# Product banks of a seven-product block: both operand parts in one 512-column matmul, and weight sums placed one product earlier

## The chip, the cores and the metric

The kernel runs on one core of a Trainium2 chip. The metric is the device time of one execution in microseconds (us), which is some 2 us longer than the span from the first instruction to the last; the median of several runs is compared. The engines are named as in the profile: PE is the matrix engine (PEld its weight loads), DVE the vector engine, ACT the scalar engine, POOL the one that issues some DMAs, SP the one that issues most of them.

## The reference, cut to what matters

One decoder block of width 2048 over 512 tokens in float32: a normed input is multiplied by `w_in`, goes through two token mixers (latent attention and a gated spatial unit), the two are merged by gates, and a dense feed-forward layer follows.

```
f = rms_norm(h, norm_ffn_g[l])
h = h + (jax.nn.silu(f @ w_gate_ffn[l]) * (f @ w_up_ffn[l])) @ w_down_ffn[l]
```

The change touches the matrix products with the columns of `w_in` that make `u` and the two gate branches, and `f @ w_gate_ffn` and `f @ w_up_ffn`, which are 2048 by 5632 each.

## The kernel before

Each of those products is cut into jobs of 256 output features. The part called x-jobs here has 20 of them (4 for `u`, 16 for the gates), the feed-forward part has 44 (gate and up in turn). A job is one `Unit`. A unit does the product by a two-by-two block scheme with seven products in place of eight (Strassen's, in Winograd's form): the weights are four quarters `a11`, `a21`, `a12`, `a22`, some of which are first added to or subtracted from one another, and the inputs stand ready as seven sums for each of eight row pairs `kp`.

Every operand is held as two parts, a high part in the matmul's own format and the rest, the low part. A product of two operands is three matmuls: low weights by high input, high weights by high input, high weights by low input. `product` issues these three for each of the eight `kp`, 24 matmuls of 256 columns, all into one PSUM bank of which 256 of the 512 columns are used (`bank`). The high and the low input lie side by side, `x[:, :256]` and `x[:, 256:]`.

A unit has three banks. Products 0 and 4 go into the first (called a below), 1, 3 and 5 into the second (b), 2 and 6 into the third (d). The banks go on accumulating, and what stands in them is read between the products: `read(0)` copies bank a to `u` (ACT), `read(1)` adds bank b and `u` to `u2` (DVE), `read(3)` makes `c22` from banks b and d (DVE, two adds), `read(4)` copies bank a to `c11` (ACT), `read(5)` makes `c12` and `read(6)` makes `c21` (DVE). After `read(6)` the job's `finish` runs: in an x-job one activation on each of two tiles (ACT), in a gate job of the feed-forward two multiplications (DVE) and two Silu (ACT), in an up job two multiplications with the gate (DVE). A product into a bank has to wait until the read of that bank before it is through.

`weights(i)` makes the weights of product i: in `form_w` ACT casts the 128x1024 sum to the high part and DVE subtracts it from the sum for the low part. Before that, where needed, DVE makes the sum itself: three sums (`s1`, `a21`, `a11`) in `weights(1)`, one (`a12`) in `weights(5)`.

`run` sets the order by hand. Every instruction of a unit is pinned to program order on its engine, and one step `g` does `read` of product g-4, `weights` of product g, and the matmuls of product g-3. DVE and ACT therefore work through one list each, step by step, and an instruction that waits holds up all that is behind it on its engine. There is room for four pairs of weight parts, so the cast of product g can start when product g-4 is through on PE.

The rest of the kernel (the products with 512 columns in `gemm_fm` and `gemm_tm`, attention, the last projection) isn't touched.

Of the kernel before, what the change touches and what calls it, by code (L numbers as in the profile page):

```python
# [88 lines left out]
def tile_block(ctx: ExitStack, tc, a):  # L89
    nc = tc.nc  # L90
# [8 lines left out]
    def T():  # L99
        return af.get(2)  # L100

    def drop(*ts):

        for t in ts:
            if isinstance(t, (tuple, list)):
                drop(*t)
            elif id(t) in af.held:
                af.put(t)
            else:
                ar.put(t)  # L110

    def PS():
        return psp.tile([P, 512], F32, tag="b", name="b")
# [183 lines left out]
    kps = PS()  # L297
    for half in range(2):
# [5 lines left out]
        for k in range(8):  # L304
            w = wk[:, k].rearrange("p o m -> p (o m)")
# [61 lines left out]
    pin = tc.keep_in_program_order  # L367

    def form_w(src):
        hi, lo = ar.get(4), ar.get(4)  # L370
        hv, lv = (t.rearrange("p (k m) -> p k m", m=P) for t in (hi, lo))
        pin(nc.scalar.copy(hv, src))  # L372
        pin(nc.vector.tensor_tensor(out=lv, in0=src, in1=hv.bitcast(F32), op=ALU.subtract))  # L373
        return hi, lo

    FORM = (0, 5, 6, 4, 1, 2, 3)

    def product(ps, w, xs, kps, first):
        hi, lo = w
        for kp in kps:  # L380
            x = xs[kp]
            ks = slice(kp * P, (kp + 1) * P)
            xh, xl = x[:, :256], x[:, 256:]
            pin(nc.tensor.matmul(ps, lo[:, ks], xh, start=first and kp == 0, stop=False, skip_group_check=True))  # L384
            pin(nc.tensor.matmul(ps, hi[:, ks], xh, start=False, stop=False, skip_group_check=True))  # L385
            pin(nc.tensor.matmul(ps, hi[:, ks], xl, start=False, stop=kp == 7, skip_group_check=True))  # L386

    def bank():
        return PS()[:, :256]

    def plus(out, in0, in1):
        pin(nc.vector.tensor_tensor(out=out, in0=in0, in1=in1, op=ALU.add))  # L392

    def minus(out, in0, in1):
        pin(nc.vector.tensor_tensor(out=out, in0=in0, in1=in1, op=ALU.subtract))  # L395

    def copy(out, t):
        pin(nc.scalar.copy(out, t))  # L398

    class Unit:  # L400
# [8 lines left out]
            self.finish = finish  # L409

        def weights(self, i):
            if i == 0:
                return form_w(self.a11)
            if i == 1:
                self.st = af.get(4)
                self.s1 = self.st.rearrange("p (k m) -> p k m", m=P)
                plus(self.s1, self.a21, self.a22)
                minus(self.a21, self.a11, self.a21)
                minus(self.a11, self.s1, self.a11)
                return form_w(self.a11)  # L420
            if i == 2:
                return form_w(self.a21)
            if i == 3:
                w = form_w(self.s1)
                drop(self.st)
                return w
            if i == 4:
                return form_w(self.a12)
            if i == 5:
                minus(self.a12, self.a12, self.a11)  # L430
                return form_w(self.a12)
            w = form_w(self.a22)
            drop(self.raw)
            return w

        def multiply(self, i, w, fx, kps):
            if i == 0 and 0 in kps:
                self.banks = [bank() for _ in range(3)]
            n = FORM[i]
            xs = [f[n] if isinstance(f, list) else f[:, n * 512:(n + 1) * 512] for f in fx]  # L440
            product(self.banks[(0, 1, 2, 1, 0, 1, 2)[i]], w, xs, kps, i < 3)

        def read(self, i):
            ba, bb, bd = self.banks
            if i == 0:
                self.out = T(), T()
                self.u = T(), T()
                copy(self.u[0][:, :256], ba)
            u, u2 = self.u[0][:, :256], self.u[1][:, :256]
            (c11, c12), (c21, c22) = ((t[:, :256], t[:, 256:]) for t in self.out)  # L450
            if i == 1:
                plus(u2, bb, u)
            elif i == 3:
                plus(c22, bb, u)
                plus(c22, bd, c22)
            elif i == 4:
                copy(c11, ba)
            elif i == 5:
                plus(c12, bb, u)
            elif i == 6:  # L460
                plus(c21, bd, u2)
                drop(self.u)
                self.finish(self.out)

    def run(jobs, fx, rest, ends, lead=3):


        af.keep, af.pack = 32, True
        jobs = list(jobs)
        last = 7 * len(jobs) - 7  # L470
        units, ready = {}, {}

        def unit(n):
            if n < len(jobs):
                units[n] = Unit(*jobs[n])

        unit(0)
        for g in range(last + 7 + lead + 1):
            g1, g2 = g - lead, g - lead - 1
            if g2 >= 0:  # L480
                units[g2 // 7].read(g2 % 7)
            if g < last + 7:
                ready[g] = units[g // 7].weights(g % 7)
                if g % 7 == 6:
                    unit(g // 7 + 2)
            if g == lead - 1:
                rest = rest()
                next(rest)
                early = len(fx)
                for i in range(lead):  # L490
                    units[0].multiply(i, ready[i], fx, range(early))
                for _ in rest:
                    pass
                unit(1)
            if 0 <= g1 < last + 7:
                if g1 == last:
                    fx[:] = [ar.cut(f, 2) for f in fx]
                units[g1 // 7].multiply(g1 % 7, ready[g1], fx, range(early if g1 < lead else 0, len(fx)))
                drop(ready.pop(g1))
                if g1 >= last:  # L500
                    drop([f[FORM[g1 - last]] for f in fx])
                    if g1 - last in ends:
                        ends[g1 - last]()
        af.keep, af.pack, ar.keep = 0, False, 0
# [28 lines left out]
    def x_rest():  # L533
# [5 lines left out]

    latT, zs = [], []  # L540
    run(x_jobs(), fx, x_rest, {0: lambda: zs.append(lat_in(0)), 2: lambda: zs.append(lat_in(1)),
                               4: lambda: latT.append(latents(0, zs[0])), 5: lambda: latT.append(latents(1, zs[1]))})
    qnT, kvT = latT
# [119 lines left out]
    def k_proj(pr):  # L663
        ch = [chunk(a["w_ukv"][pr, c]) for c in range(2)]
        ks = []
        for m in range(2):
            ps = PS()
            for k in range(4):
                hi, lo = ch[k // 2]
                o = (k % 2) * 512 + m * P  # L670
                mm3(ps, hi[:, o:o + P], lo[:, o:o + P], *kvT[k], k == 0, k == 3)
            ks.append(split(ps))
        return ks, ch
# [63 lines left out]
    def values(e, pts, vs):  # L737
        ps = PS()
        for j, (ph, pl, q0) in enumerate(pts):
            vh, vl = vs[j // 2]  # L740
            o = (j % 2) * 256 + e * P
            mm3(ps[:, q0:], vh[:, o:o + P], vl[:, o:o + P], ph, pl, j == 0, j == NB - 1)
        return ps
# [15 lines left out]
    ks, ch = k_proj(0)  # L759
    vs = v_proj(ch)  # L760
    for pr in range(NP):
        prob, ptiles = scores(qs, qp, ks)
        if pr + 1 < NP:
            qs, qp = q_proj(pr + 1)
            ks, ch = k_proj(pr + 1)
# [12 lines left out]
        for e in range(2):  # L778
            ps = values(e, pts[e][1], vs)
            t = T()  # L780
# [60 lines left out]
    for c in range(4):  # L841
# [30 lines left out]
        if c == 0:  # L872
# [3 lines left out]
            for tb in range(NB):  # L876
                t = T()
# [56 lines left out]
    def split_hidden():  # L934
        hid[:4] = [move(t) for t in hid[:4]]

    run(ffn_jobs(), ff, f_rest, {1: lambda: hid.extend(hidden_in(0, 4)), 4: split_hidden,
                                 5: lambda: hid.extend(hidden(4, 4))})

# [32 lines left out]
    for c in range(4):  # L972
        t = T()
# [3 lines left out]
    for tb in range(NB):  # L977
        ts = slice(tb * P, (tb + 1) * P)
        for c in range(4):
            ps = PS()  # L980
            for k in range(4):
                xh, xl = hid[k]
# [6 lines left out]
        for c in range(4):  # L989
            t = h[tb][c]  # L990
# [87 lines left out]
```

## Time and profile before

| | |
|---|---|
| median of 3 runs | 2736.05 us (2734.65 to 2737.57) |
| the profiled execution, its own time | 2731.94 us |
| its span, first to last instruction | 2729.9 us |
| mean granted TensorE clock | 0.993 |
| PE busy | 2679.5 us, 98% of the span |
| DVE busy | 1731.3 us, 63% |
| ACT busy | 1093.6 us, 40% |
| instructions on PE | 17320 matmuls, of which 10752 are those of `product` |

The busy share of an engine is a mean over parts with different limits. A matmul's duration in the profile runs from its start to the modelled end, and the next one starts before that end, so the cost of a matmul in a row of them is the distance between two starts. In the timelines the start stands first, then the time that the group took; behind "x2" two neighbours of one form are merged. In brackets stands how long the engine was idle before and what released it.

### The profile page before, as it was taken

Reading aid. Unit: us, or ns where it says so; the run is one execution under the profiler, and the core shown is the slowest. Engines: PE = TensorE matmul, PEld = TensorE weight load, DVE = VectorE, ACT = ScalarE, POOL = GpSimd, SP = SyncE. Lnnn points to the kernel's source line nnn. Section 1 sums busy time; section 2 is a strip of 40 time slices with the busy share of each in tenths; the row PEclk is TensorE's granted clock in tenths of the full one; section 3 lists DMA queues with packets and bytes.
Section 4 is the critical chain, followed back from the end, with each engine's and each line's share of the span. In section 5 each row is a group of like instructions: output and inputs, shape, how many; then the busy total and the mean of one; then the engine's idle time right before and its main releaser. Section 6 shows DMA issues by size and latency. Waiting matters only on the chain.

```text
span 2729.9 us, 41675 instructions
## 1 busy us (share of the span) xinstructions
PE 2679.5 (98%) x17320; PEld 2458.8 (90%) x17320; DVE 1731.3 (63%) x2200; ACT 1093.6 (40%) x1534; POOL 201.4 (7%) x377
## 2 busy tenths in 40 slices
PE   8999999999899999999999999999999999999998
PEld 6879999998789878888799999999999998888887
DVE  5647777787677433333687887887888875344434
ACT  6334444457456422233544443444444343222212
POOL 1000000011101220001000000000000020000000
PEclk9999999999999999999999999999999999999999
DMA  7433343343423754334233232332322356334321
GB/s 300 150 125 114 119 146 125 130 144 129 139 86 124 250 188 147 120 112 139 101 123 118 110 131 109 131 111 107 140 109 109 132 170 224 123 123 132 112 89 62
DMA packets 104540, 365.22 MB, mean 134 GB/s; under 512 B 14304, under 2 KB 14304, under 8 KB 104352
## 3 DMA queue, kind: packets, MB, share of 16 engines
q1 hardware_dynamic: 72720, 260.60, 27.2%
q0 software_dynamic: 30192, 99.38, 10.6%
q8 instruction: 135, 2.21, 0.3%
q10 hardware_dynamic: 1440, 2.60, 0.3%
q14 instruction: 53, 0.43, 0.1%
HBM read 317.17 MB, written 45.35 MB: 133 GB/s over the span
## 4 chain that ended last, share of the span: by engine, by line
PE 82%; issue 9%; DMA 4%; DVE 3%; ACT 1%; POOL 1%; SPq 0%; POOLq 0%; ACTq 0%; DVEq 0%
PE b L384 15%; PE b L386 15%; PE b L385 15%; PE b L169 12%; PE b L171 12%; PE b L170 12%; DMA af<-in_xT 1%; DVE ar L373 1%; DMA af<-in_w_uq 1%; ACT ar L372 1%; DVE af L395 0%; PE b L732 0%; DVE af L392 0%; DMA sgd<-af 0%; DMA af<-in_w_lat 0%
## 5 line engine op out<-in xcount | busy, mean ns | idle before, releaser
L384 PE MATMUL b<-ar 128*128 128x256 f32 x3584 | 1017.6, 284 | 6.6 <-ACT ar L333 3.4
L386 PE MATMUL b<-ar 128*128 128x256 f32 x3584 | 1017.2, 284 | 5.4 <-DVE ar L119 5.4
L385 PE MATMUL b<-ar 128*128 128x256 f32 x3584 | 1016.5, 284 | 0.0
L169 PE MATMUL b<-ar 128*128 128x512 f32 (+1 forms) x2016 | 766.3, 380 | 25.3 <-ACT ar L154 11.6
L171 PE MATMUL b<-ar 128*128 128x512 f32 (+1 forms) x2016 | 763.8, 379 | 0.3 <-DVE ar L155 0.3
L170 PE MATMUL b<-ar 128*128 128x512 f32 (+1 forms) x2016 | 764.0, 379 | 0.0
L373 DVE TENSOR_TENSOR ar<-af,ar 128x1024 fp32r<-128x1024 f32 x448 | 543.2, 1223 | 267.9 <-ACT ar L372 266.9
L384 PEld LDWEIGHTS b<-ar 128*128 128x128 f32 x3584 | 690.5, 193 | 7.9 <-DVE af L392 4.0
L386 PEld LDWEIGHTS b<-ar 128*128 128x128 f32 x3584 | 690.5, 193 | 6.3 <-DVE ar L119 6.3
L385 PEld LDWEIGHTS b<-ar 128*128 128x128 f32 x3584 | 690.7, 193 | 0.1
L372 ACT CAST ar<-af 128x1024 fp32r<-128x1024 f32 x448 | 458.5, 1047 | 479.8 <-DVE af L395 367.9
L155 DVE TENSOR_TENSOR ar<-af,ar 128x1024 fp32r<-128x1024 f32 (+1 forms) x224 | 268.2, 1204 | 423.5 <-ACT ar L154 347.4
L169 PEld LDWEIGHTS b<-ar 128*128 128x128 f32 x2016 | 380.5, 189 | 97.6 <-ACT ar L154 11.9
L171 PEld LDWEIGHTS b<-ar 128*128 128x128 f32 x2016 | 380.2, 189 | 71.5 <-DVE ar L155 1.5
L170 PEld LDWEIGHTS b<-ar 128*128 128x128 f32 x2016 | 380.6, 189 | 69.6
L154 ACT CAST ar<-af 128x1024 fp32r<-128x1024 f32 (+1 forms) x224 | 230.0, 1036 | 503.0 <-PE b L170 241.6
L395 DVE TENSOR_TENSOR af<-af 128x1024 f32<-128x1024 f32 x192 | 234.6, 1222 | 4.3
L392 DVE TENSOR_TENSOR af<-b,af 128x256 f32<-128x256 f32 x320 | 134.3, 420 | 14.3 <-PE b L386 12.1
L137 ACT CAST ar<-af 128x512 fp32r<-128x512 f32 x100 | 59.6, 620 | 180.1 <-PE b L170 43.7
L398 ACT COPY af<-b 128x256 f32<-128x256 f32 x128 | 47.4, 370 | 178.8 <-PE b L386 132.5
L138 DVE TENSOR_TENSOR ar<-af,ar 128x512 fp32r<-128x512 f32 x100 | 67.2, 687 | 71.5 <-ACT ar L137 67.7
L942 DVE SCALAR_TENSOR_TENSOR af<-b,rest,af 128x512 f32<-128x512 f32 x96 | 71.3, 748 | 44.5 <-PE b L171 44.5
(223 smaller groups left out, 1193.5 us busy)
## 6 DMA issues: line engine op xcount, KB each, us to landing
af<-in_w_gate SPq DMA_DIRECT2D x88, 512.0 KB, 4.9
af<-in_w_up SPq DMA_DIRECT2D x88, 512.0 KB, 5.3
af<-in_w_down SPq DMA_DIRECT2D x88, 512.0 KB, 3.5
af<-in_w_g SPq DMA_DIRECT2D x64, 512.0 KB, 5.4
af<-in_w_oattn SPq DMA_DIRECT2D x32, 512.0 KB, 4.2
af<-in_w_out SPq DMA_DIRECT2D x32, 512.0 KB, 3.5
hidd<-af POOLq DMA_DIRECT2D x44, 256.0 KB, 2.6
af<-hidd POOLq DMA_DIRECT2D x44, 256.0 KB, 3.6
```

The source lines that it names most:

```text
L154: nc.scalar.copy(hi[:, :n], raw[:, :n])
L155: nc.vector.tensor_tensor(out=lo[:, :n], in0=raw[:, :n], in1=hi[:, :n].bitcast(F32), op=ALU.subtract)
L169: nc.tensor.matmul(ps, sl, mh, start=first, stop=False)
L170: nc.tensor.matmul(ps, sh, mh, start=False, stop=False)
L171: nc.tensor.matmul(ps, sh, ml, start=False, stop=last)
L372: pin(nc.scalar.copy(hv, src))
L373: pin(nc.vector.tensor_tensor(out=lv, in0=src, in1=hv.bitcast(F32), op=ALU.subtract))
L384: pin(nc.tensor.matmul(ps, lo[:, ks], xh, start=first and kp == 0, stop=False, skip_group_check=True))
L385: pin(nc.tensor.matmul(ps, hi[:, ks], xh, start=False, stop=False, skip_group_check=True))
L386: pin(nc.tensor.matmul(ps, hi[:, ks], xl, start=False, stop=kp == 7, skip_group_check=True))
L392: pin(nc.vector.tensor_tensor(out=out, in0=in0, in1=in1, op=ALU.add))
L395: pin(nc.vector.tensor_tensor(out=out, in0=in0, in1=in1, op=ALU.subtract))
```

## The change

`product` gets the bank's number and, where `WIDE` says so for that bank (it does for all three), makes two matmuls in place of three: the high weights by the whole 512 columns of input, which leaves high by high in the left half of the bank and high by low in the right half, and the low weights by the high input into the left half. `bank()` goes, a unit takes whole banks. As a bank now holds its result in two halves, `add` reads both: where one DVE add stood there are two, the second with the result of the first; where an ACT copy stood there is the copy of the right half and a DVE add of the left one. `u` and `u2` now share one tile.

`weights` makes the sums of product i+1 right behind the cast and the subtraction of product i: `s1`, `a21` and `a11` in step 0 in place of step 1, `a12` in step 4 in place of step 5.

```
-    def product(ps, w, xs, kps, first):
+    WIDE = (True, True, True)
+
+    def product(b, ps, w, xs, kps, first):
...
-            pin(nc.tensor.matmul(ps, lo[:, ks], xh, start=first and kp == 0, stop=False, skip_group_check=True))
-            pin(nc.tensor.matmul(ps, hi[:, ks], xh, start=False, stop=False, skip_group_check=True))
-            pin(nc.tensor.matmul(ps, hi[:, ks], xl, start=False, stop=kp == 7, skip_group_check=True))
-
-    def bank():
-        return PS()[:, :256]
+            start, stop = first and kp == 0, kp == 7
+            if WIDE[b]:
+                pin(nc.tensor.matmul(ps, hi[:, ks], x, start=start, stop=False, skip_group_check=True))
+                pin(nc.tensor.matmul(ps[:, :256], lo[:, ks], xh, start=False, stop=stop, skip_group_check=True))
...
         def weights(self, i):
+
             if i == 0:
-                return form_w(self.a11)
-            if i == 1:
+                w = form_w(self.a11)
                 self.st = af.get(4)
                 self.s1 = self.st.rearrange("p (k m) -> p k m", m=P)
                 plus(self.s1, self.a21, self.a22)
                 minus(self.a21, self.a11, self.a21)
                 minus(self.a11, self.s1, self.a11)
-                return form_w(self.a11)
...
+            elif i == 4:
                 minus(self.a12, self.a12, self.a11)
...
+        def add(self, out, b, t=None):
+
+            ps = self.banks[b]
+            if t is not None:
+                plus(out, ps[:, :256], t)
+            if t is None and not WIDE[b]:
+                copy(out, ps[:, :256])
+            elif t is None:
+                copy(out, ps[:, 256:])
+                plus(out, ps[:, :256], out)
+            elif WIDE[b]:
+                plus(out, ps[:, 256:], out)
```

On PE one product of a unit begins like this before the change, the rows of one `kp` under those of another (`b` is the bank, `ar` the weights and inputs):

```order
L384 MATMUL b<-ar 128x256
L385 MATMUL b<-ar 128x256
L386 MATMUL b<-ar 128x256
L384 MATMUL b<-ar 128x256
L385 MATMUL b<-ar 128x256
L386 MATMUL b<-ar 128x256
```

and like this after it:

```order
L389 MATMUL b<-ar 128x512
L390 MATMUL b<-ar 128x256
L389 MATMUL b<-ar 128x512
L390 MATMUL b<-ar 128x256
L389 MATMUL b<-ar 128x512
```

For each `kp` three matmuls of 256 columns became one of 512 and one of 256.

On DVE, in the feed-forward, from the reads of product 3 (`read(3)`) to the two multiplications of the `finish` of a gate job; L392 with `b` on the right is a read of a bank, L373 the subtraction for low weights, L395 and the L392 of 128x1024 are the weight sums, L908 the multiplications. Before:

```order
L392 TENSOR_TENSOR af<-b,af 128x256 x2
L373 TENSOR_TENSOR ar<-af,ar 128x1024
L392 TENSOR_TENSOR af<-af 128x1024
L395 TENSOR_TENSOR af<-af 128x8x128 x2
L373 TENSOR_TENSOR ar<-af,ar 128x1024
L392 TENSOR_TENSOR af<-b,af 128x256
L373 TENSOR_TENSOR ar<-af,ar 128x1024
L392 TENSOR_TENSOR af<-b,af 128x256
L908 TENSOR_TENSOR af<-af,rxb 128x512 x2
```

After, in the same piece, L398 is the adding of reads and of `s1`, L401 the other sums, L922 the multiplications:

```order
L398 TENSOR_TENSOR af<-b,af 128x256 x4
L373 TENSOR_TENSOR ar<-af,ar 128x1024
L398 TENSOR_TENSOR af<-af 128x1024
L401 TENSOR_TENSOR af<-af 128x8x128 x2
L398 TENSOR_TENSOR af<-b,af 128x256
L373 TENSOR_TENSOR ar<-af,ar 128x1024
L398 TENSOR_TENSOR af<-b,af 128x256 x2
L373 TENSOR_TENSOR ar<-af,ar 128x1024
L398 TENSOR_TENSOR af<-b,af 128x256 x2
L922 TENSOR_TENSOR af<-af,rxb 128x512 x2
```

Four bank reads became nine here, and one of the new ones (for `c11`) stands between the sums and the next subtraction.

On DVE, from those multiplications to the subtraction of product 6, before:

```order
L908 TENSOR_TENSOR af<-af,rxb 128x512 x2
L373 TENSOR_TENSOR ar<-af,ar 128x1024 x2
L392 TENSOR_TENSOR af<-b,af 128x256
L395 TENSOR_TENSOR af<-af 128x8x128
L373 TENSOR_TENSOR ar<-af,ar 128x1024 x2
```

and after:

```order
L922 TENSOR_TENSOR af<-af,rxb 128x512 x2
L373 TENSOR_TENSOR ar<-af,ar 128x1024
L398 TENSOR_TENSOR af<-b,af 128x256
L373 TENSOR_TENSOR ar<-af,ar 128x1024
L401 TENSOR_TENSOR af<-af 128x8x128
L398 TENSOR_TENSOR af<-b,af 128x256 x2
L373 TENSOR_TENSOR ar<-af,ar 128x1024 x2
```

The read of bank b into `u2`, one row before, is two rows now and stands behind the sum `a12`; one row for `u` is new.

## Rows read from the trace of the kernel before

**Rows 1.** The page, part 1: busy us (share of the span) xinstructions of each engine.

```profile
PE 2679.5 (98%) x17320; PEld 2458.8 (90%) x17320; DVE 1731.3 (63%) x2200; ACT 1093.6 (40%) x1534; POOL 201.4 (7%) x377
```

**Rows 2.** Groups by line and form: xcount | busy us, mean ns | idle before.

```profile
L384 PE MATMUL b<-ar 128*128 128x256 f32 x3584 | 1017.6, 284 | 6.6 <-ACT ar L333 3.4 <-DVE af L392 3.2
...
L169 PE MATMUL b<-ar 128*128 128x512 f32 x1792 | 699.9, 391 | 15.7 <-ACT ar L154 11.6 <-DVE ar L155 4.2
```

**Rows 3.** Busy by stretch (x-jobs, feed-forward); PE, PEld, DVE, ACT, POOL, clock, DMA, GB/s.

```profile
330.00:480.00 150.00, 150.00 (x1252) 150.00 (x1251) 110.17 (x120) 68.00 (x83) 8.65 (x16) 1.00 0.35 127
...
1400.00:1900.00 500.00, 500.00 (x4169) 500.00 (x4169) 399.15 (x447) 205.78 (x248) 12.85 (x24) 1.00 0.33 120
```

**Rows 4.** Timeline of PE, 1100 to 1108 us, two of a row of 512-column matmuls.

```profile
1099.97 0.39 PE L171 MATMUL b<-ar 128*128 128x512 f32 x1
...
1106.77 0.39 PE L171 MATMUL b<-ar 128*128 128x512 f32 x1
```

**Rows 5.** Timeline of all engines, 421.3 to 422.3 us, the end of a product 3.

```profile
421.46 0.28 PE L386 MATMUL b<-ar 128*128 128x256 f32 x1
...
421.78 0.89 DVE L392 TENSOR_TENSOR af<-b,af 128x256 f32<-128x256 f32 x2 [0.52 <-PE b L386]
```

**Rows 6.** Timeline of DVE, 1474 to 1493 us, a unit behind an up job.

```profile
1474.40 1.23 DVE L373 TENSOR_TENSOR ar<-af,ar 128x1024 fp32r<-128x1024 f32 x1 [1.17 <-ACT ar L372]
1475.54 0.42 DVE L392 TENSOR_TENSOR af<-b,af 128x256 f32<-128x256 f32 x1
1475.88 1.22 DVE L373 TENSOR_TENSOR ar<-af,ar 128x1024 fp32r<-128x1024 f32 x1
...
1477.34 1.28 DVE L916 TENSOR_TENSOR af<-af 128x512 f32<-128x512 f32 x2
1478.55 1.22 DVE L373 TENSOR_TENSOR ar<-af,ar 128x1024 fp32r<-128x1024 f32 x1
...
1487.38 0.88 DVE L392 TENSOR_TENSOR af<-b,af 128x256 f32<-128x256 f32 x2
1488.45 1.22 DVE L373 TENSOR_TENSOR ar<-af,ar 128x1024 fp32r<-128x1024 f32 x1 [0.20 <-ACT ar L372]
1489.60 1.22 DVE L392 TENSOR_TENSOR af<-af 128x1024 f32<-128x1024 f32 x1
1490.85 2.48 DVE L395 TENSOR_TENSOR af<-af 128x1024 f32<-128x1024 f32 x2
```

**Rows 7.** Timeline of DVE, 1450 to 1500 us, behind a gate job's multiplications.

```profile
1457.18 1.28 DVE L908 TENSOR_TENSOR af<-af,rxb 128x512 f32<-128x512 f32 x2
1460.10 2.44 DVE L373 TENSOR_TENSOR ar<-af,ar 128x1024 fp32r<-128x1024 f32 x2 [1.64 <-ACT ar L372]
```

**Rows 8.** Timeline of DVE, 408.9 to 416.6 us, behind an x-job's last read.

```profile
411.63 0.41 DVE L392 TENSOR_TENSOR af<-b,af 128x256 f32<-128x256 f32 x1
413.77 2.44 DVE L373 TENSOR_TENSOR ar<-af,ar 128x1024 fp32r<-128x1024 f32 x2 [1.73 <-ACT ar L372]
```

**Rows 9.** Timeline of all engines, 212.9 to 215.6 us, in the first x-job.

```profile
214.90 0.42 DVE L392 TENSOR_TENSOR af<-b,af 128x256 f32<-128x256 f32 x1
...
215.38 0.58 PE L384 MATMUL b<-ar 128*128 128x256 f32 x1 [2.04 <-DVE af L392]
```

**Rows 10.** The page, part 6: DMA issues, KB each, us to landing.

```profile
af<-in_w_gate SPq DMA_DIRECT2D x88, 512.0 KB, 4.9
```

**Rows 11.** Timeline of PE, 753.8 to 756.8 us, a restart after an idle piece.

```profile
756.08 0.39 PE L169 MATMUL b<-ar 128*128 128x256 f32 x1 [1.80 <-DVE nm L712]
756.30 0.28 PE L170 MATMUL b<-ar 128*128 128x256 f32 x1
```

**Rows 12.** Timeline of PE, 994 to 998 us.

```profile
997.39 0.79 PE L169 MATMUL b<-ar 128*128 128x512 f32 x1 [3.24 <-DVE ar L155]
```

**Rows 13.** Busy by stretch behind those two idle pieces, columns as in rows 3.

```profile
756.10:759.50 3.40, 3.40 (x21) 3.16 (x22) 1.82 (x8) 2.12 (x7) 0.54 (x1) 1.00 0.93 264
...
997.30:1000.70 3.40, 3.31 (x8) 2.64 (x9) 1.17 (x2) 0.00 (x0) 0.00 (x0) 0.51 0.68 216
```

More of the change, by code (lines that the diff above doesn't have):

```diff
@@ L383, in product @@
             xh, xl = x[:, :256], x[:, 256:]
-            pin(nc.tensor.matmul(ps, lo[:, ks], xh, start=first and kp == 0, stop=False, skip_group_check=True))
-            pin(nc.tensor.matmul(ps, hi[:, ks], xh, start=False, stop=False, skip_group_check=True))
-            pin(nc.tensor.matmul(ps, hi[:, ks], xl, start=False, stop=kp == 7, skip_group_check=True))
-    def bank():
-        return PS()[:, :256]
+            start, stop = first and kp == 0, kp == 7
+            if WIDE[b]:
+                pin(nc.tensor.matmul(ps, hi[:, ks], x, start=start, stop=False, skip_group_check=True))
+                pin(nc.tensor.matmul(ps[:, :256], lo[:, ks], xh, start=False, stop=stop, skip_group_check=True))
+            else:
+                ps = ps[:, :256]
+                pin(nc.tensor.matmul(ps, lo[:, ks], xh, start=start, stop=False, skip_group_check=True))
+                pin(nc.tensor.matmul(ps, hi[:, ks], xh, start=False, stop=False, skip_group_check=True))
+                pin(nc.tensor.matmul(ps, hi[:, ks], xl, start=False, stop=stop, skip_group_check=True))
     def plus(out, in0, in1):
@@ L419, in weights @@
                 minus(self.a11, self.s1, self.a11)
-                return form_w(self.a11)
-            if i == 2:
-                return form_w(self.a21)
+                return w
+            w = form_w((None, self.a11, self.a21, self.s1, self.a12, self.a12, self.a22)[i])
             if i == 3:
-                w = form_w(self.s1)
                 drop(self.st)
[L426 to L429, printed above, removed]
+            elif i == 4:
                 minus(self.a12, self.a12, self.a11)
-                return form_w(self.a12)
-            w = form_w(self.a22)
-            drop(self.raw)
+            elif i == 6:
+                drop(self.raw)
             return w
@@ L437, in multiply @@
             if i == 0 and 0 in kps:
-                self.banks = [bank() for _ in range(3)]
+                self.banks = [PS() for _ in range(3)]
             n = FORM[i]
             xs = [f[n] if isinstance(f, list) else f[:, n * 512:(n + 1) * 512] for f in fx]
-            product(self.banks[(0, 1, 2, 1, 0, 1, 2)[i]], w, xs, kps, i < 3)
+            b = (0, 1, 2, 1, 0, 1, 2)[i]
+            product(b, self.banks[b], w, xs, kps, i < 3)
+        def add(self, out, b, t=None):
[9 more added lines that the diff above has]
+                plus(out, ps[:, 256:], out)
         def read(self, i):
-            ba, bb, bd = self.banks
             if i == 0:
[L446 to L449, printed above, removed]
+                self.out, self.us = (T(), T()), T()
+            u, u2 = self.us[:, :256], self.us[:, 256:]
             (c11, c12), (c21, c22) = ((t[:, :256], t[:, 256:]) for t in self.out)
-            if i == 1:
-                plus(u2, bb, u)
+            if i == 0:
+                self.add(u, 0)
+            elif i == 1:
+                self.add(u2, 1, u)
             elif i == 3:
-                plus(c22, bb, u)
-                plus(c22, bd, c22)
+                self.add(c22, 1, u)
+                self.add(c22, 2, c22)
             elif i == 4:
-                copy(c11, ba)
+                self.add(c11, 0)
             elif i == 5:
-                plus(c12, bb, u)
+                self.add(c12, 1, u)
             elif i == 6:
-                plus(c21, bd, u2)
-                drop(self.u)
+                self.add(c21, 2, u2)
+                drop(self.us)
                 self.finish(self.out)
```

## The prediction

> **What bounds the kernel now.** I read the page's first part, then the busy time by stretch, then the timelines of PE, DVE and ACT through single units. PE is busy for 98% of the span, DVE for 63%, ACT for 40% [rows 1]. By stretch the picture is sharper: inside the units PE never stops, neither in the x-jobs nor in the feed-forward, at a clock of 1.00, and DVE is busy for 110 of 150 us and for 399 of 500 us [rows 3]. So in the units PE sets the pace and DVE has a fifth to a quarter to spare. The 284 ns of a 256-column matmul [rows 2] aren't its cost; 1252 matmuls in 150 us and 4169 in 500 us [rows 3] are 0.120 us each. A product of 24 matmuls thus takes 2.88 us, a unit of seven products 20.16 us.
>
> DVE's spare time isn't free to use at any moment, though. Its timeline shows one list of work in fixed order, with waits for casts of ACT in it (1.17, 1.64 and 1.73 us) [rows 6 to 8]. And there is one place where PE already waited on DVE: in the first x-job the read of bank b was late, it ended at 215.32, and the product behind it, idle for 2.04 us, started 0.06 us later [rows 9]. This is the wait that the change must be priced by.
>
> **What it does on PE.** Thirty distances between 512-column matmuls take 6.80 us [rows 4], 0.2267 us each; a 256-column one is 0.120. Twice the columns cost less than twice the time, so each matmul carries 2 x 0.120 - 0.2267 = 0.0133 us that doesn't depend on its columns. One `kp` goes from 3 x 0.120 = 0.360 to 0.2267 + 0.120 = 0.3467 us, a product from 2.88 to 2.773, a unit from 20.16 to 19.41 us. Over the 3584 `kp` [rows 2] that is 47.8 us, if nothing else becomes late.
>
> The rows' fixed part is 13.3 ns. The Trainium skill ("TensorE: Matmul & The Clock Gate", section "Wait — 56ns, not 53.3ns?") gives a fixed cost of about 2.5 ns for each matmul at the full clock, measured with bf16; by it the same 3584 removed matmuls would save an estimated 9.0 us. The rows here, with float32 parts, disagree with it, and I go by the rows.
>
> **What it does on DVE.** A unit had 5 bank reads on DVE and 2 copies on ACT; now it has 12 on DVE and the 2 copies. Seven more at 0.34 us (from 1475.54 to 1475.88) [rows 6], or 0.45 where a read needs the one before it (the pair of 0.88 us is 0.42 + 0.46), are about 3 us in a unit. The feed-forward's DVE goes from 399/500 x 20.16 = 16.1 to some 19 us in a unit that PE would like to do in 19.41. That total would just fit, but the order decides. A bank may not be written while it is read. Bank b is read by `read(1)`, between product 1 and product 3, with only product 2 in between; so the second row of `u2` holds up product 3, and on DVE it stands behind everything from `read(3)` of the unit before. I follow the list from the start of product 3 to the start of the next unit's product 3, behind an up job:
>
> Product 3 itself 2.77. To its first read 0.20 (the last matmul starts at 421.46, the next product 0.12 later, the read at 421.78) [rows 5]. Four reads for `c22`, three at 0.45 and one at 0.34, 1.69. Subtraction for product 0, 1.15. Sums `s1`, `a21`, `a11`, each waiting for the one before, 1.25 + 1.25 + 1.23 = 3.73 [rows 6]. Then DVE waits 1.17 for the cast of `a11`, as it does now [rows 6]: the sums stand a step earlier, but directly ahead of the cast that needs them, with only the new read of `c11` (0.34) in the wait. Subtraction for product 1, 1.14. Two reads for `c12`, 0.79. Subtraction for product 2, 1.14. Two reads for `c21`, 0.79. Two multiplications, 1.21 (1477.34 to 1478.55) [rows 6]. Subtraction for product 3, 1.14. Read of `u`, 0.34. Subtraction for product 4 and the sum `a12` that overwrites its source, 1.25 + 1.14. Two reads for `u2`, 0.45 + 0.42. To the start of product 3, 0.06 [rows 9]. A restart of PE costs 0.10 more than a matmul in a row (0.22 from 756.08 to 756.30 against 0.12) [rows 11]. The sum is **20.68 us**, 0.52 over the 20.16 of before: PE's own seven products (19.41) no longer set the unit.
>
> Behind a gate job, Silu stands between the multiplications and the cast for product 3 on ACT. From the start of the multiplications to the subtraction it takes 2.92 us [rows 7] and not 1.21, so the loop is 1.71 longer, 22.39. Behind an x-job it is the activation on both tiles: 2.14 from the last read to the subtraction [rows 8] against 0.34 + 1.21, 0.60 longer, 21.28. Before the change all these waits ended before product 3 was due. The sum `a12`, moved ahead, does its work: its cast's wait no longer counts. The two subtractions behind `u2` (products 5 and 6) run beside product 3.
>
> In total 22 up jobs at 0.52, 22 gate jobs at 2.23 and 20 x-jobs at 1.12 make 11.4 + 49.1 + 22.4 = **82.9 us more**. The reordered loads and the shared tile of `u` I cost at nothing: a unit's weights are asked for a unit ahead, some 20 us, and a load lands 4.9 us after its issue [rows 10]; without that cover a unit would wait for its first cast.
>
> **What the clock adds.** PE now stands still ahead of each product 3. By the profile's count, from the modelled end of the last matmul (0.16 later than its slot), a gate job's pause is 22.39 - 19.41 - 0.10 - 0.16 = 2.72 us, an x-job's 1.61, an up job's 1.01. In the rows an idle piece of 1.80 us [rows 11] was followed by a stretch at full clock, one of 3.24 us [rows 12] by 3.40 us at 0.51 of it [rows 13], the level of 1.2 GHz, in which 1.7 us of work is lost. That work would be product 3, which lies in the loop. 2.72 is 0.64 of the way from 1.80 to 3.24, so I take the fall in 14 of the 22 gate jobs: 23.8 us. Its bounds are 0 and all 22 (37 us).
>
> **Sum.** The profiled execution took 2731.94 us; 2731.94 + 82.9 + 23.8 = 2838.6. It lay 4.1 us under the median of the runs, so on the median's scale 2842.8; I say **2843 us**.
>
> **Rivals.** (A) PE sets the pace after all and the full 47.8 us come off: 2688 us. For it: DVE's total of some 19 us fits into 19.41. Against it: the loop would have to be 1.27 us shorter even behind an up job, and its terms are rows. It decides at a loop of 19.41. (B) The clock stays up through the pauses: 2736.05 + 82.9 = 2819 us. For it: 2.72 us is shorter than the one single pause that was followed by a fall. (C) The clock falls behind the x-jobs' pauses of 1.61 us too, 42 units x 1.7 = 71 us: 2736.05 + 82.9 + 71 = 2890 us. Against it: the 1.80 us of [rows 11]. The Trainium skill's section "A second HAM failure mode: psum-queue depth-cycling" (same page) describes this: short pauses between groups of matmuls that cycle through PSUM banks made the clock swing; no run here yet shows it for pauses so short. (D) The moved sums do hide the cast of `a11`, and the 1.17 us leave the loop: 19.51, 21.22 and 20.11 for up, gate and x, which is -0.65 x 22 + 1.06 x 22 - 0.05 x 20 = +8: 2744 us. Against it: the cast still needs the last sum, and DVE's next row but one needs the cast.
>
> **How the numbers follow.** The forecast has 0.48, B 0.24, C 0.12, D 0.07, A 0.09. A measurement of this kernel can tell about 0.2% (5.5 us) from no change. All but A, and some of D, lie above that: slower 0.87, within 0.2% 0.04, faster 0.09. The range takes in forecast, B and C and leaves A and D out (0.16): from 2800, which is B with 0.3 us less in each of 64 loops, to 2890.
>
> **What would show it.** Right: the new matmuls start 0.227 and 0.120 us after one another; in the feed-forward PE has one pause in each unit, at its product 3, released by DVE's bank reads, of some 1 and 3 us in turn; units last about 20.7 and 22.4 us in turn, and 21.3 in the x-jobs; DVE is busy for around 90%; behind some long pauses the granted clock shows 0.5. Wrong: PE without pauses inside the units (A), pauses but a clock of 1.00 (B), half clock in the x-jobs (C), no wait of DVE for the cast behind the sums (D), or a 512-column matmul that takes more than 0.227 us beside a 256-column one.

## The result, and the profile after

The changed kernel takes 2932.05 us (2930.57 to 2936.6 in four runs), the kernel before 2736.81 beside it: a ratio of 1.0718, with a 95% interval of 1.0701 to 1.0735. It is slower, as forecast, but by 195 us and not by 107, outside the range. The span of the profiled execution grew from 2729.9 to 2934.4 us.

The page after, part 1 (busy us, share of the span, instructions; answers to [rows 1]) and three groups of part 5 (answer to [rows 2]):

```profile
PE 2731.0 (93%) x13736; PEld 2321.3 (79%) x13736; DVE 1910.3 (65%) x2648; ACT 1090.6 (37%) x1534; POOL 201.5 (7%) x377
...
L389 PE MATMUL b<-ar 128*128 128x512 f32 x3584 | 1333.2, 413 | 151.7 <-DVE af L398 142.4
L390 PE MATMUL b<-ar 128*128 128x256 f32 x3584 | 1035.9, 289 | 0.0
...
L398 DVE TENSOR_TENSOR af<-b,af 128x256 f32<-128x256 f32 x768 | 324.0, 422 | 124.1 <-PE b L390 100.5
```

PE has 3584 matmuls fewer, DVE 448 instructions more, and the wide matmul L389 stood idle for 142.4 us behind L398, the bank reads; before, that wait was 3.2 us [rows 2]. By stretch (columns as in [rows 3]; the x-jobs, then the feed-forward):

```profile
330.00:480.00 150.00, 138.88 (x787) 119.75 (x787) 123.75 (x162) 63.36 (x78) 7.57 (x14) 1.00 0.33 123
1550.00:2050.00 500.00, 447.51 (x2357) 384.98 (x2358) 398.91 (x529) 175.63 (x213) 10.81 (x20) 0.93 0.27 99
```

PE is no longer busy throughout, in either part. In these stretches the clock is 1.00 for the x-jobs and 0.93 for the feed-forward. The timeline of DVE over one loop behind a gate job, from the reads of product 3 to the subtractions beside the next one (answers to [rows 6, 7]):

```profile
1603.42 1.80 DVE L398 TENSOR_TENSOR af<-b,af 128x256 f32<-128x256 f32 x4 [2.03 <-PE b L390]
1605.13 1.22 DVE L373 TENSOR_TENSOR ar<-af,ar 128x1024 fp32r<-128x1024 f32 x1
1606.26 1.22 DVE L398 TENSOR_TENSOR af<-af 128x1024 f32<-128x1024 f32 x1
1607.52 2.48 DVE L401 TENSOR_TENSOR af<-af 128x1024 f32<-128x1024 f32 x2
1609.92 0.42 DVE L398 TENSOR_TENSOR af<-b,af 128x256 f32<-128x256 f32 x1
1611.17 1.23 DVE L373 TENSOR_TENSOR ar<-af,ar 128x1024 fp32r<-128x1024 f32 x1 [0.84 <-ACT ar L372]
...
1615.03 1.28 DVE L922 TENSOR_TENSOR af<-af,rxb 128x512 f32<-128x512 f32 x2
1617.95 1.23 DVE L373 TENSOR_TENSOR ar<-af,ar 128x1024 fp32r<-128x1024 f32 x1 [1.63 <-ACT ar L372]
...
1621.82 0.88 DVE L398 TENSOR_TENSOR af<-b,af 128x256 f32<-128x256 f32 x2
1623.09 2.36 DVE L373 TENSOR_TENSOR ar<-af,ar 128x1024 fp32r<-128x1024 f32 x2 [0.40 <-ACT ar L372]
```

And PE's timeline where the last two reads (`u2`) end: an x-job, a unit behind a gate job, a unit behind an up job.

```profile
391.26 0.47 PE L389 MATMUL b<-ar 128*128 128x512 f32 x1 [1.72 <-DVE af L398]
...
1622.84 0.47 PE L389 MATMUL b<-ar 128*128 128x512 f32 x1 [2.82 <-DVE af L398]
...
1624.36 0.63 PE L389 MATMUL b<-ar 128*128 128x512 f32 x1
...
1627.28 0.40 PE L389 MATMUL b<-ar 128*128 128x512 f32 x1
...
1646.38 0.47 PE L389 MATMUL b<-ar 128*128 128x512 f32 x1 [2.30 <-DVE af L398]
```

The pair of reads ends at 1622.70, product 3 starts at 1622.84, and at 1627.28 product 4: product 3 took 4.44 us where 2.77 is its time at full clock (granted clock 0.62 over it; 0.50, the level of 1.2 GHz, from 1624 to 1626). The wide matmul at 1624.36 shows 0.63 us where it shows 0.40 at the full clock. Between two products 3 lie 24.04 us behind a gate job (from 1598.80, the start of the one before, to 1622.84) and 23.54 behind an up job (1622.84 to 1646.38).

### The profile page after: what moved, and what is told of

It is laid out like the page before. It is cut to its first block, busy times and chain, and to the rows that moved or that the text cites. A ratio compares the mean times of both kernels' runs of the same rounds, so it can differ in the third digit from the quotient of the medians.

```text
span 2934.4 us, 35138 instructions
## 1 busy us (share of the span) xinstructions
PE 2731.0 (93%) x13736; PEld 2321.3 (79%) x13736; DVE 1910.3 (65%) x2648; ACT 1090.6 (37%) x1534; POOL 201.5 (7%) x377
## 5 line engine op out<-in xcount | busy, mean ns | idle before, releaser
L389 PE MATMUL b<-ar 128*128 128x512 f32 x3584 | 1333.2, 413 | 151.7 <-DVE af L398 142.4
L390 PE MATMUL b<-ar 128*128 128x256 f32 x3584 | 1035.9, 289 | 0.0
L389 PEld LDWEIGHTS b<-ar 128*128 128x128 f32 x3584 | 708.5, 198 | 339.9 <-issue 152.6
L390 PEld LDWEIGHTS b<-ar 128*128 128x128 f32 x3584 | 712.9, 199 | 0.1
L373 DVE TENSOR_TENSOR ar<-af,ar 128x1024 fp32r<-128x1024 f32 x448 | 541.4, 1221 | 167.7 <-ACT ar L372 167.5
L169 PEld LDWEIGHTS b<-ar 128*128 128x128 f32 x2016 | 381.4, 189 | 109.3 <-DVE nm L726 15.4
L171 PEld LDWEIGHTS b<-ar 128*128 128x128 f32 x2016 | 381.1, 189 | 73.1 <-DVE ar L155 2.4
L170 PEld LDWEIGHTS b<-ar 128*128 128x128 f32 x2016 | 381.3, 189 | 69.8
L398 DVE TENSOR_TENSOR af<-b,af 128x256 f32<-128x256 f32 x768 | 324.0, 422 | 124.1 <-PE b L390 100.5
L401 DVE TENSOR_TENSOR af<-af 128x1024 f32<-128x1024 f32 x192 | 235.2, 1225 | 6.5
L165 POOL DMA_DIRECT2D hidd<-af x44 | 23.8, 541 | 989.4 <-DVE af L930 988.2
L398 DVE TENSOR_TENSOR af<-af 128x1024 f32<-128x1024 f32 x64 | 78.0, 1219 | 0.0
```

Of the source, the lines that this page charges most:

```text
L169: nc.tensor.matmul(ps, sl, mh, start=first, stop=False)
L170: nc.tensor.matmul(ps, sh, mh, start=False, stop=False)
L171: nc.tensor.matmul(ps, sh, ml, start=False, stop=last)
L389: pin(nc.tensor.matmul(ps, hi[:, ks], x, start=start, stop=False, skip_group_check=True))
L390: pin(nc.tensor.matmul(ps[:, :256], lo[:, ks], xh, start=False, stop=stop, skip_group_check=True))
```

## The experiments

All times are medians beside runs of the kernel before on the same chip (2736 to 2738 us there). "The loop" is the prediction's: from one product 3 to the next, along DVE's list.

**Reads of the right half left out** (the product of high weights by low input is missing from the result).

```
             ps = self.banks[b]
             if t is not None:
                 plus(out, ps[:, :256], t)
-            if t is None and not WIDE[b]:
+            else:
                 copy(out, ps[:, :256])
-            elif t is None:
-                copy(out, ps[:, 256:])
-                plus(out, ps[:, :256], out)
-            elif WIDE[b]:
-                plus(out, ps[:, 256:], out)
```

> This kernel keeps the wide matmuls but reads only the left half of each bank (the product of high weights by low input is left out of the result), with as many reads as before the change. Loop theory (DVE's list between two products 3 sets the unit, through the reads of bank b): without the seven added reads the loop falls below PE's 19.41 us, PE has no pauses inside the units, the clock stays at 1.00 there, and the time is 2736 - 48 = about 2688 us. Rival (the wide matmul itself is dear, or two forms in turn stop PE): the units stay longer than 20.16 us with PE busy throughout, and the time stays above 2736.

It took 2733.18 us, 0.9984 of before (0.9975 to 0.9993). Against the changed kernel's 2932 that is 199 us less: the seven added reads are thus worth all of the 195 us, by way of what follows from them. But the 48 us of gain aren't there either. Its x-jobs by stretch, and then the timeline of all engines around a product 3 in the feed-forward:

```profile
330.00:480.00 150.00, 150.00 (x851) 130.12 (x850) 113.85 (x122) 69.99 (x84) 8.58 (x16) 1.00 0.35 128
```

```profile
1605.31 0.42 DVE L398 TENSOR_TENSOR af<-b,af 128x256 f32<-128x256 f32 x1
...
1605.87 0.47 PE L389 MATMUL b<-ar 128*128 128x512 f32 x1 [0.22 <-DVE af L398]
```

In this stretch of the x-jobs PE doesn't stop, and yet 851 matmuls take 150 us. From unit to unit it is 19.79 us, or 0.3533 for a pair, not 0.3467; only the three x-jobs ahead of the stretch, also without a pause, went at 0.3467 (19.41 us a unit). In the feed-forward the read of bank b, one row only, still comes too late behind the sum `a12`, and units last 20.02 us on average. The expectation that the loop falls below 19.41 missed: the sum of 22.39 behind a gate job less the seven reads (five at 0.45, one at 0.34, and that of `c11`, which stood in a wait) is 19.80, and 20.16 was measured there, 19.88 behind an up job.

**Only the weight sums a step earlier**: `WIDE = (False, False, False)`. The shared tile of `u` stays, too.

> This kernel has WIDE false for all three banks: the three matmuls and the single reads of before, with only the weight sums a step earlier. Loop theory: DVE has room, units last 20.16 us, 2736 to 2742 us. Rival (moving the sums ahead of the next reads is what makes the reads late): 20 us or more above 2736.

2749.43 us, 1.0039 (1.0024 to 1.0054). Its units last 20.16 in the x-jobs and 20.22 in the feed-forward, 3 us in all; the other 10 lie outside the steady units. So the moved sums and the shared tile cost little by themselves, and they gain nothing.

**The pauses filled**: eight matmuls into a fourth bank ahead of each product 3.

```
-                self.banks = [PS() for _ in range(3)]
+                self.banks = [PS() for _ in range(4)]
...
+            if i == 3:
+                for _ in range(8):
+                    pin(nc.tensor.matmul(self.banks[3], w[0][:, :P], xs[0], start=True, stop=True, skip_group_check=True))
```

> The changed kernel, with eight 512-column matmuls into a fourth bank that nobody reads put ahead of each product 3 (1.81 us, less than the pauses of 1.9 to 3.0 us there). Loop theory: they fill the pauses, DVE's loop stays what it is, and the clock no longer falls in the 44 feed-forward units: 44 x 1.67 = 73 us less than the changed kernel's 2932, about 2859, with loops of 21.9 and 22.4 us in turn. If the clock falls for another reason than the pauses, or the half clock costs nothing on the loop: 2932 or more (up to 64 x 1.81 = 116 us more).

2871.36 us, 1.0481 (1.0464 to 1.0499), 61 us less than the changed kernel, with 512 more matmuls. Its timeline of PE at the same place, and its feed-forward by stretch:

```profile
1635.01 2.03 PE L444 MATMUL b<-ar 128*128 128x512 f32 x8
1637.07 0.50 PE L389 MATMUL b<-ar 128*128 128x512 f32 x1
...
1640.00 0.40 PE L389 MATMUL b<-ar 128*128 128x512 f32 x1
```

```profile
1550.00:2050.00 500.00, 491.71 (x2709) 418.17 (x2708) 426.33 (x564) 185.00 (x224) 11.91 (x22) 1.00 0.29 109
```

Product 3 takes 2.93 us and the clock is 1.00. The loops are 22.46 behind a gate job (predicted without the clock: 22.39) and 21.94 behind an up job (predicted 20.68). So the half clock was worth about 1.6 us on each loop that it fell in, some 67 us for the 42 of 44 feed-forward units in which it fell; that 61 were gained goes with a stretch between the two parts that is 6 us longer here. 1.2 us behind up jobs are something else.

**u in another place**: the three result tiles taken in another order from the arena.

```
-                self.out, self.us = (T(), T()), T()
+                first, self.us, second = T(), T(), T()
+                self.out = second, first
```

> The changed kernel with the tiles of a unit's results taken in another order, so that u gets another place and ACT's copy into it waits less often for DVE's subtraction for product 3 (which still reads the place it had). Loop theory with that wait as the missed term: the loops behind up jobs fall from 23.5 to some 22.4 us where the wait goes, and to 20.7 where the shorter pause then keeps the clock up: 22 x 1.2 = 26 up to 22 x 2.85 = 63 us less than 2932, 2869 to 2906. If the copy's wait isn't on the loop: 2932.

2915.2 us, 1.0646 (1.0626 to 1.0666), 17 us less than the changed kernel, and 9 us above the range expected. The missing 1.2 us are in ACT's and DVE's timelines of the changed kernel behind an up job:

```profile
1640.29 1.22 DVE L373 TENSOR_TENSOR ar<-af,ar 128x1024 fp32r<-128x1024 f32 x1
1642.01 0.42 DVE L398 TENSOR_TENSOR af<-b,af 128x256 f32<-128x256 f32 x1 [0.49 <-ACT af L404]
1642.95 1.22 DVE L373 TENSOR_TENSOR ar<-af,ar 128x1024 fp32r<-128x1024 f32 x1 [0.52 <-ACT ar L372]
```

```profile
1641.60 0.37 ACT L404 COPY af<-b 128x256 f32<-128x256 f32 x1 [4.50 <-DVE ar L373]
```

The copy into `u` waits for the end of the subtraction for product 3 (1641.51), most likely since `u` is given the place that this subtraction reads (the run with another order bears that out below); the read of `u` waits for the copy, and the cast of product 4 stands behind the copy on ACT. From one subtraction to the next it is 2.66 us and not 1.48, 1.18 more. The same wait stood in ACT's timeline before the change, where it delayed nothing:

```profile
1479.85 0.37 ACT L398 COPY af<-b 128x256 f32<-128x256 f32 x1 [2.89 <-DVE ar L373]
```

In the kernel with the other order the wait is gone behind every second up job, eleven in all, and there PE's pause is short:

```profile
1705.50 0.51 PE L389 MATMUL b<-ar 128*128 128x512 f32 x1 [2.83 <-DVE af L398]
...
1727.83 0.47 PE L389 MATMUL b<-ar 128*128 128x512 f32 x1 [1.10 <-DVE af L398]
...
1984.03 0.47 PE L389 MATMUL b<-ar 128*128 128x512 f32 x1 [2.46 <-DVE af L398]
...
2004.83 0.47 PE L389 MATMUL b<-ar 128*128 128x512 f32 x1 [0.79 <-DVE af L398]
```

22.33 us from the first to the second, with a product 3 of 4.43 us in it: with 2.77 in its place 20.67, the predicted loop (20.68). From the third to the fourth the clock stayed up all the way, and the loop is 20.80 as measured. All eleven short pauses lasted 0.61 to 1.10 us, and behind each of them product 3 took 2.85 to 2.89 us at a clock of 1.00. Behind the other ten up jobs the pauses grew to 2.5 to 3.2 us, since there the copy into `u` waits for the store of the up job's result:

```profile
1676.66 0.37 ACT L404 COPY af<-b 128x256 f32<-128x256 f32 x1 [5.39 <-DMA hidd<-af]
```

**One bank wide**: `WIDE = (True, False, False)`, bank a, and `(False, True, False)`, bank b.

> WIDE true for bank a alone: products 0 and 4 take two matmuls for each kp, u and c11 get one DVE read more each, banks b and d are read as before the change. Loop theory: two reads (0.34 each) more on DVE's list from one product 3 to the next; with the sum a12 ahead of the read of bank b this just reaches PE's pace behind feed-forward jobs (20.3 us a unit) and stays below it in the x-jobs (20.0): 2736 to 2745 us. Rival (each added read costs its share of the 196 us, whichever bank it is of, 2 of 7): 2736 + 56 = 2792.

> WIDE true for bank b alone: products 1, 3 and 5, three added reads, all of bank b. Loop theory: the reads lie on the loop, and the pair for u2 ends it: 21.2 us a unit in the feed-forward and 20.2 in the x-jobs, pauses of about 1 us and a clock that stays up: 44 x 1.0 = 45 us, 2781. Rival (a share of the 196 us by reads, 3 of 7): 2736 + 84 = 2820. Against bank a alone the loop theory says nine times its cost, the rival one and a half times.

Bank a: 2745.17 us, 1.003 (1.0018 to 1.0043). Bank b: 2800.02 us, 1.023 (1.0215 to 1.0246). Seven us against 62, nine times as much for three added reads as for two: what counts is where a read stands on the list that ends at bank b. The units with bank b wide last 20.42 in the x-jobs and 21.20 in the feed-forward (expected 20.2 and 21.2); some 10 us more lie outside the units.

**A fourth bank** for products 3 and 5, so that product 3 waits for no read; with bank a wide, and with all banks wide.

```
-                self.banks = [PS() for _ in range(3)]
+                self.banks = [PS() for _ in range(4)]
...
-            b = (0, 1, 2, 1, 0, 1, 2)[i]
+            b = (0, 1, 2, 3, 0, 3, 2)[i]
-            product(b, self.banks[b], w, xs, kps, i < 3)
+            product(b, self.banks[b], w, xs, kps, i < 4)
...
-                self.add(c22, 1, u)
+                self.add(c22, 3, u2)
...
-                self.add(c12, 1, u)
+                self.add(c12, 3, u2)
```

> WIDE true for bank a alone, and products 3 and 5 go into a fourth bank of their own (c22 and c12 are then made from u2 and that bank), so that product 3 no longer waits for the read of bank b. As many reads on DVE as with bank a alone. Loop theory: the wait ahead of product 3 goes; units are PE's own 19.95 to 20.05 us, with 0.353 to 0.347 us for a pair of matmuls: 8 to 13 us less than before, 2723 to 2728. If the wait for bank b isn't what held PE there: as with bank a alone, 2739 or more.

> The kernel of the run four_w100 once more, in more rounds: bank a wide, products 3 and 5 in a fourth bank. Loop theory: 64 x 0.107 = 6.8 us less than before at 0.353 us a pair, 2729 to 2731 us.

> The fourth bank for products 3 and 5 and the sums in their new steps, but WIDE false for all banks: three matmuls for each kp everywhere. It tells whether the 6 us that the fourth bank with bank a wide takes off come from the two-matmul products or from the fourth bank. Loop theory: PE sets the pace at 20.16 us a unit, 2736 us, as before. If the fourth bank itself gains: 2730.

> All banks wide, and products 3 and 5 in a fourth bank, so that product 3 waits for no read. Loop theory: the wait ahead of product 3 goes, but DVE's list with its own waits for ACT is longer than PE's 19.41 to 19.75 us, so PE now waits a product or two later, for the reads of bank a ahead of product 4 (and of the fourth bank ahead of product 5): 21.7 us a unit in the feed-forward and 20.8 in the x-jobs, 44 x 1.53 + 20 x 0.64 + 14 = 2736 + 94 = 2830 us with pauses of 1.0 to 1.9 us and a clock that mostly stays up; 2900 where it falls. If bank b's wait were the whole cost: 2736 - 25 = 2711.

With bank a wide: 2732.3 us, 0.9982 (0.9972 to 0.9991), and in the second set 2732.37, 0.9985 (0.9976 to 0.9994): 4 to 6 us faster than the kernel before, 0.2%. Its steady units last 20.05 us in both parts, PE's own 5 x 2.88 + 2 x 2.83. That is as expected, and the time still missed its range (2723 to 2728, then 2729 to 2731): in the profiled execution the stretch between the last x-job and the first feed-forward unit took 736.5 us instead of 731.0. With all narrow it is 2737.74, 1.0006 (0.9997 to 1.0015): the fourth bank alone gains nothing. The groups of the first show how little PE still waits for reads (2.0 us, L393):

```profile
L393 PE MATMUL b<-ar 128*128 128x256 f32 x2560 | 726.6, 284 | 2.0 <-DVE af L398 2.0
...
L389 PE MATMUL b<-ar 128*128 128x512 f32 x1024 | 369.3, 400 | 8.8 <-DVE ar L119 8.8
```

With all banks wide: 2829.6 us, 1.034 (1.0324 to 1.0355), 102 us less than the changed kernel. The units last 20.91 and 21.68 us (expected 20.8 and 21.7), and the mean granted clock is 0.991. The wait has moved, not to bank a but to the fourth bank: product 5 has to wait for the reads of that bank, the first two of the four for `c22`.

```profile
1698.95 0.47 PE L389 MATMUL b<-ar 128*128 128x512 f32 x1 [1.40 <-DVE af L398]
```

So the bank was the place of the wait, and the length of DVE's list, with its own waits, is its cause.

**The sums back in their old steps**, all banks wide.

```
             if i == 0:
-                w = form_w(self.a11)
+                return form_w(self.a11)
+            if i == 1:
                 self.st = af.get(4)
...
-                return w
+            if i == 5:
+                minus(self.a12, self.a12, self.a11)
             w = form_w((None, self.a11, self.a21, self.s1, self.a12, self.a12, self.a22)[i])
...
-            elif i == 4:
-                minus(self.a12, self.a12, self.a11)
```

> The changed kernel with the weight sums back in their old steps (three sums in step 1, a12 in step 5, behind the read of bank b), WIDE true for all banks. Loop theory: a12 (1.25) leaves the list ahead of product 3, but behind it stand now a12, a wait of 1.2 for its cast and two subtractions, 4.7 us, more than product 3's 2.97 at full clock, and the read of c11 no longer fills DVE's wait for the cast of a11: 22.7 us a unit in the feed-forward and 21.8 in the x-jobs. Product 3 at half the clock (4.4 us) is then hidden beside these 4.7 us, 23.0 at most: 44 x 2.55 to 2.85 + 20 x 1.65 to 1.95 + 14 outside the units = 2895 to 2915 us. If the moved sums are what makes the change dear: 2860 or less. If they help as much as they would in a list without waits: 2932 + 64 x 1.2 = over 3000.

2918.6 us, 1.0665 (1.0648 to 1.0683), some 13 us less than with the moved sums and 4 us above the range expected. Units last 22.09 and 23.02 us. Without the clock this order has the longer loop (22.93 us behind a gate job, where 22.52 was measured with the moved sums); with it, it is the cheaper one. Behind a product 3 at half clock that loop is 23.43, 0.5 us longer and not 1.5: DVE has more to do beside product 3, and the half clock there is hidden in part. And the clock fell less often, in 20 of 40 feed-forward units (22 to 61, counted from the first x-job as unit 0) against 38: thirteen of the pauses were only 1.44 to 1.73 us long, and seven of 2.92 to 3.28 us left it up, too. Behind this one product 4 starts 2.89 us later:

```profile
1487.81 0.47 PE L389 MATMUL b<-ar 128*128 128x512 f32 x1 [3.28 <-DVE af L398]
...
1490.70 0.40 PE L389 MATMUL b<-ar 128*128 128x512 f32 x1
```

**The sums on POOL**: the four weight sums of a unit go to the engine that is idle.

```
-                plus(self.s1, self.a21, self.a22)
+                plus(self.s1, self.a21, self.a22, nc.gpsimd)
...
-                minus(self.a12, self.a12, self.a11)
+                minus(self.a12, self.a12, self.a11, nc.gpsimd)
```

> The changed kernel with the four weight sums of a unit on POOL in place of DVE, 5 us less on DVE's list in each unit. Loop theory: the loop of an up job falls from 21.9 by 3.7 (three sums) and 1.1 (a12) to 17 us, below PE's 19.41, provided that POOL takes less than two products (5.5 us) for three sums and doesn't slow DVE: 2688 to 2700 us. If POOL is slow (over 3 us a sum) or shares its way to memory with DVE: the loop stays and the time is anywhere from 2736 to over 2932. Rival (PE's matmuls are dear): no gain, 2900 or more.

3031.27 us, 1.1073 (1.1056 to 1.1089), the slowest of all. Timelines of POOL and of DVE in that kernel:

```profile
1621.17 2.39 POOL L401 TENSOR_TENSOR af<-af 128x1024 f32<-128x1024 f32 x1 [10.73 <-DVE ar L373]
1623.52 2.41 POOL L398 TENSOR_TENSOR af<-af 128x1024 f32<-128x1024 f32 x1
1626.01 3.22 POOL L401 TENSOR_TENSOR af<-af 128x1024 f32<-128x1024 f32 x1
```

```profile
1620.95 0.87 DVE L398 TENSOR_TENSOR af<-b,af 128x256 f32<-128x256 f32 x2
1624.67 5.64 DVE L373 TENSOR_TENSOR ar<-af,ar 128x1024 fp32r<-128x1024 f32 x2 [2.85 <-ACT ar L372]
```

A sum takes POOL 2.4 to 3.2 us where DVE takes 1.22, and two of DVE's subtractions that run beside it take 5.64 us instead of 2.36. Ahead of them DVE waits 2.85 us for a cast that itself waited for POOL's sum. The list got longer instead of shorter: units last 24.1 and 25.0 us. DVE's groups over the whole kernel:

```profile
L373 DVE TENSOR_TENSOR ar<-af,ar 128x1024 fp32r<-128x1024 f32 x448 | 745.9, 1676 | 478.2 <-ACT ar L372 478.2
L398 DVE TENSOR_TENSOR af<-b,af 128x256 f32<-128x256 f32 x768 | 322.6, 420 | 26.9 <-ACT af L404 10.9 <-PE b L390 3.1
```

## Why the prediction was wrong, point by point

- **What bounds it, and where it waits: right.** PE's pauses inside the units lie ahead of product 3, released by DVE's bank reads, as forecast. Leaving the added reads out, giving product 3 another bank, and widening bank b alone or bank a alone each moved the time as that wait demands. DVE's work came out as forecast, too: 398.91 of 500 us at 23.7 us a unit are 18.9 us, "some 19"; its share is 80% and not 90% because the units last longer.
- **PE's price: a term was mis-sized.** I took 0.3467 us for a pair from rows of 512-column matmuls among themselves [rows 4] and of 256-column ones. In the changed kernel many products do cost that (product 0 at 1611.54, product 1 at 1614.31), others 0.3533 a pair; with the added reads left out, all but the first x-jobs cost 0.3533. At that price the gain without any wait would have been 3584 x 0.0067, some 24 us, and not 48; the forecast didn't rest on it. What a matmul less saves is 13.3 or 6.7 ns in these rows. Both are more than the 2.5 ns that the Trainium skill ("TensorE: Matmul & The Clock Gate", section "Wait — 56ns, not 53.3ns?") gives for bf16.
- **The loop behind gate jobs: right, term by term.** 22.39 was the sum; 22.46 was measured with the pauses filled, and 22.52 in the changed kernel itself behind the two product 3 that kept the full clock; 24.04 with the half clock in it.
- **The loop behind up jobs: a missed wait of 1.18 us, the first step that failed.** The sum of 20.68 follows DVE's list, and the step "Subtraction for product 3, 1.14. Read of `u`, 0.34" has in it that `u` is ready. It isn't: the copy into it waits for that very subtraction, which ACT's timeline before the change already names as releaser. That wait stood there with two tiles for `u` and `u2` as well, so the shared tile isn't its cause; what is new is that DVE's list now has a read of `u` right behind the copy. Where the wait was gone, the loop was the predicted one (20.80, or 20.67 when set to the full clock). By itself it cost 22 x 1.18 = 26 us.
- **The clock: the second step that failed.** "I take the fall in 14 of the 22 gate jobs" was a value between two bounds. It fell behind all 22 gate jobs, and in 20 of the other 22 feed-forward units, where the forecast had none; 28 more falls x 1.67 = 47 us. The 20 are for the most part a consequence of the missed wait: with 1.18 us more, the pauses behind up jobs were 2.0 to 2.3 us and not 1.01, and in the kernel where the wait was gone behind eleven up jobs the clock stayed up behind all eleven. So the missed wait carries 26 us and, with the 19 falls behind up jobs, some 32 more; the gate jobs' eight falls are 13.
- **That the pause's length decides** was the premise of those 14, and it holds in part only. In all fourteen traces together (pauses of 0.5 us and more in the units, without the first unit of each part), none of 210 pauses up to 1.75 us was followed by half clock, and 161 of 183 longer ones were. But a pause of 1.95 us was (the 19th x-job of the changed kernel), two of 2.2 us there were not, nor were seven of about 3 us with the sums in their old steps. What else decides stays open.
- **The loop behind x-jobs: nearly right.** 21.28 predicted, 21.28 to 21.43 measured in the steady units; with the first and the last x-jobs it is 6 us in all.
- **Rival C**, the clock in 42 units, was right in the number of falls by chance and wrong in the place: not the x-jobs but the up jobs. The Trainium skill's section "A second HAM failure mode: psum-queue depth-cycling" ("TensorE: Matmul & The Clock Gate") describes a clock that swings with pauses between groups of matmuls that cycle through PSUM banks; the feed-forward, with its 42 falls behind pauses of 2 us and more, agrees with it, and the x-jobs' pauses of 1.3 to 1.7 us don't.
- **Outside the units.** From the start of the x-jobs' last product to the first matmul of the feed-forward's units it took 744.7 us instead of 731.0, 13.7 more, and from their last product to the end 2.1 more. In other experiments the same stretch varied between 730 and 751 us, in most of them longer than before. Why wasn't tested, and it stays open.

Together 26 + 47 + 6 + 16 = 95 us. The profiled execution, from which all these are read, took 2936.6 us where 2838.6 was the sum for it, 98 more.

## What to carry to other kernels

Before work is shifted from a full engine to one with a fifth to spare, follow the second one's list from one hand-over to the next, with its waits: the sum of its work (18.9 us) fitted here into PE's 19.41, the loop through one bank didn't. In such a walk every operand needs its own releaser, also the ones that end harmlessly early now (the copy into `u`), and tiles that come out of an arena inherit the waits of their last reader. Where a wait opens a pause on PE, price the pause with the half clock behind it as the likely case once it is longer than those that never brought the clock down (up to 1.75 us in these traces), and see whether what runs slower then lies on the loop: a fall made the loop behind a gate job 1.5 us longer with the moved sums, and 0.5 with the old ones.

## What the runs showed of the hardware that I hadn't expected

- Pairs of a 512- and a 256-column matmul settle at one of two costs, 0.3467 or 0.3533 us, both at a granted clock of 1.00. Both are found in stretches with pauses and in stretches without. Why isn't known.
- Pauses of PE of 2.0 to 2.8 us, once in a unit of some 24 us, were followed by half clock (1.2 GHz) in 40 of the 42 feed-forward units 20 to 61, counted from the first x-job as unit 0; the first such pause there, at 3.65 us, was longer: product 3 took 4.2 us or more (once 5.3) in place of 2.77. Behind pauses of 1.3 to 1.7 us, in 17 x-job units one after the other, it took 2.85 to 2.90. Length alone doesn't settle it: with the sums in their old steps seven pauses of about 3 us left the clock at 1.00.
- POOL's additions slow DVE's: the subtraction L373, which reads two operands from SBUF, went from 1.22 to 1.68 us on average, while the bank reads L398, which read one from PSUM, stayed at 0.42. The Trainium skill ("GPSIMD Engine Reference", section "Specifications") says that POOL's SBUF interfaces are shared with VectorE, with contention for instructions with two SBUF inputs; the two rows agree.
